# Layer two of two feed-forward parts: where its first rows and operands lie, and which products come last

## The chip, the cores and the metric

The kernel runs on one core of one Trainium2 chip. The metric is the time of one execution on the device in microseconds (us). Only the one core is used, so nothing is exchanged with other cores.

## The reference, cut to what matters

Three transformer-like layers follow each other on a 1024 x 1024 activation in float32. The second ends with a gated feed-forward part, the third with a squared-ReLU one, each followed by a layer norm over the rows (1024 columns):

```python
# second layer
gate_ff, up_ff = jnp.split(x @ w_ffn_in, 2, axis=-1)          # 1024 -> 2 x 2816
ffn = (jax.nn.silu(gate_ff) * up_ff) @ w_ffn_out              # 2816 -> 1024
ple = jax.nn.sigmoid(x @ w_ple_gate) * (p_i @ w_ple_proj)
return _layer_norm(ALPHA * x + ffn + ple, ln2_g, ln2_b)
# third layer begins with x = layer_norm(x, ln_in_g, ln_in_b); its feed-forward part:
ff = jnp.square(jax.nn.relu(jnp.einsum('btd,df->btf', x, w1[l]) + b1[l]))   # 1024 -> 4096
ff = jnp.einsum('btf,fd->btd', ff, w2[l]) + b2[l]                            # 4096 -> 1024
x = layer_norm(DEEPNORM_ALPHA * x + ff, ln2_g[l], ln2_b[l])
```

## The kernel before

Every float32 operand is split into a high and a low part, and each product of two tiles is three matmuls (high by high, high by low, low by high). ScalarE (ACT) makes the high part with a cast, VectorE (DVE) the low one with a subtraction (`part`, L111 and L112, or L485 and L486). The queue of SyncE (SP) issues nearly all DMAs in order.

Both matrix products of a feed-forward part are made by a Winograd scheme: seven half-size products in place of eight, from sums of quarters.

Layer one is `wino_up`. For each unit of 256 columns it makes products 6, 2, 7, 5, 4, 3 and the next unit's 1. Its left operands are the quarters of the activation, which lie in the four tiles of `tpool`, and the sums S1 to S4. S2 and S3 lie in a zone of their own on the right side of SBUF (`Q.zone`, 32 KB a partition) and are read by products 6 and 7; S4, on the left with the staging tiles `h` and `snap`, is read by product 3. The results go through `sink` and `left_parts` to DRAM as `hid`: the seven left operands of layer two, unit by unit.

Layer two is `Down`. The units are taken in groups: 4, 4 and 3 units in the second layer, four groups of 4 in the third. Within a group the products go in the order 1, 6, 7, 4, 5, 3, 2 (`ORDER`). One product is four pieces, one for each 128 rows, of 12 matmuls (9 in the group of 3). A piece accumulates in one PSUM bank. Products 1, 6, 7 and 4 go on in the same four banks, 5 and 3 in four others, 2 in new ones, and after each piece `evict` adds the bank into `acc[m]`: the eight output tiles of 128 rows by 1024 columns. `TO` says which: rows 0 to 3 get products 1, 6, 3 and 2, rows 4 to 7 get 7, 4 and 5. In the last group the pieces of 4 and 5 alternate, as do those of 3 and 2, and the last addition to a row block starts its layer norm: `ln_out` once in the third layer, twice in the second (its own norm, then the norm that the third layer begins with), followed by the transposes into `T5` (L106).

The right operands come from four tiles a, b, c, d for each pair of units (`load`, L616, `ra0` to `rd1`). `combine` forms the sums in place (L440 to L444), and `split` makes the two parts: `a` for product 1, then b := d - b and a := b + a for product 6, b for 7, b := c - a for 4, a := d - a for 5, d for 3 and c for 2. Six weight buffers (`wpool`) hold three products' worth. The left operands are loaded by `left` (L587) from `hid` into raw buffers, two units at a time, and split into a tile of `tpool`. Every second pair goes through a raw buffer of `pl`; in the second layer that is one buffer, which the layer norm's `junk` shares.

At the change-over from layer one to layer two, `early` loads operands of product 1 while the last unit runs, and `later`, called when product 7 of the last unit has freed the zone, loads a to d of group 0 into it. The `acc` tiles lie on the left, where `h`, S4 and `snap` lay, and `fetch` fills them with a DMA from GpSimd's queue (L1618, L2387). In the first addition (L1623, L2399) DVE reads both the bank and `acc`, and the bank's next product waits for it.

The order of the instructions on each engine is fixed when the kernel is built, by a list scheduler that goes by program order and its own estimate of when things are ready. Hence matmuls of product 1 of layer two stand between those of the last unit's products.

Of the kernel before, what the change touches and what calls it, by code (L numbers as in the profile page):

```python
# [10 lines left out]
F32 = mybir.dt.float32  # L11
# [9 lines left out]
D = 1024  # L21
P = 128
NT = S // P
# [8 lines left out]
class Core:  # L32
# [150 lines left out]
def run(gen):  # L183
    for _ in gen:
        pass
# [377 lines left out]
class Down:  # L563
# [42 lines left out]
    def load(self, g):  # L606
        nc, pool = self.c.nc, self.pool
        u0, u1 = self.groups[g]
        parts = [{} for _ in range(u0, u1, 2)]
        for names in ("dba", "c") if g == 0 else ("adbc",):  # L610
            for x, u in enumerate(range(u0, u1, 2)):
                k = min(2, u1 - u)
                for n in names:
                    j, o = {"d": (1, 1), "b": (1, 0), "a": (0, 0), "c": (0, 1)}[n]
                    t = pool.tile([P, 2, 512], F32, name=f"r{n}{x}", tag=f"r{n}{x}", bufs=1)[:, :k]
                    nc.sync.dma_start(t, self.src[j][:, 2 * u + o:2 * (u + k):2])  # L616
                    parts[x][n] = t
        return parts

    def right(self, g):  # L620

        c, nc = self.c, self.c.nc
        parts = self.parts if g == 0 else self.load(g)
        sums = [combine(nc, *(q[n] for n in "abcd")) for q in parts]
# [24 lines left out]

    def run(self, raws, fetch, evict):  # L650

        nc = self.c.nc
        self.raws = raws
        seen = set()
        nG = len(self.groups)
        todo = [(g, n) for g in range(nG) for n in self.ORDER]

        def ahead(i):
            if i < len(todo):
                g, n = todo[i]  # L660
                if (g, n) not in self.A:
                    self.A[g, n] = self.left(n, *self.groups[g])

        def piece(g, n, x, A, W, ps):
            cs = slice(x * P, (x + 1) * P)
            row, j = self.TO[n]
            for k, (wh, wl) in enumerate(W):
                ah, al = A[:, k, cs], A[:, 4 + k, cs]
                nc.tensor.matmul(ps[x], ah, wh, start=n in (1, 5, 2) and k == 0, stop=False, skip_group_check=True)  # L669
# [6 lines left out]
        i = 0  # L676
        fetched = set()
        for g in range(nG):
            rights = self.right(g)
            pair = []  # L680
            for n in self.ORDER:
                W = next(rights)
                ahead(i)
                ahead(i + 1)
                A = self.A.pop((g, n))
                if self.TO[n] not in fetched:
                    fetched.add(self.TO[n])
                    for x in range(4):
                        fetch(4 * self.TO[n][0] + x, self.TO[n][1])
                if n in (1, 5, 2):  # L690
                    new = self.banks()
                if n in (1, 6, 7):
                    ps = new
                if g == nG - 1 and n in (4, 5, 3, 2):

                    pair.append((n, A, W, new if n != 4 else ps))
                    if len(pair) == 2:
                        for x in range(4):
                            for n, A, W, to in pair:
                                piece(g, n, x, A, W, to)  # L700
                        pair = []
                else:
                    for x in range(4):
                        piece(g, n, x, A, W, new if n != 4 else ps)
                i += 1


def block1(c, i, x1_out):
# [751 lines left out]
def block2(c, i, T, x1_scr, x3_scr):  # L1460

    nc, tc = c.nc, c.tc
# [6 lines left out]
    xs_scr = c.dram.tile([NT, P, D], F32, name="xs2", tag="xs2")  # L1469
    ys_scr = c.dram.tile([NT, P, D], F32, name="ys2", tag="ys2")  # L1470
# [21 lines left out]
    def pool(stack, name, side="left", bufs=1):  # L1492
        return stack.enter_context(tc.tile_pool(reuse_waits="tile", name=name, bufs=bufs, side=side))

    with ExitStack() as ctx:
# [52 lines left out]
        down = Down(c, i["w2_ffn_out"], hid, [(0, 4), (4, 8), (8, NFF2)])  # L1548

        def gate(j, halves):  # L1550
# [14 lines left out]
                    nc.sync.dma_start(ys_scr[m][:, cs], x)  # L1565
            return [lambda h=h: steps(h) for h in halves]

        second = []

        def before(whole):  # L1570
# [11 lines left out]
        def sink(v, C):  # L1582
# [18 lines left out]
            else:  # L1601
                have.setdefault("hidden", {})

        wino_up(c, lambda v: i["w2_ffn_in"][v // 2][:, :, 256 * (v % 2):256 * (v % 2) + 256], 0, 2 * NFF2, Q, sink,
                before, meanwhile, down.early, lambda: down.later(pool(ctx, "b2r", "right")))
        uctx.close()

        pl = pool(ctx, "b2l")
        po = pool(ctx, "b2o")
        pa = pool(ctx, "b2a")  # L1610
# [5 lines left out]
        def fetch(m, j):  # L1616
            cs = slice(j * 512, (j + 1) * 512)
# [620 lines left out]
def block3(c, i, T, x3_scr, out):  # L2238
    nc, tc = c.nc, c.tc
# [3 lines left out]
    with ExitStack() as ctx:  # L2243
# [77 lines left out]

    xs_scr = c.dram.tile([NT, P, D], F32, name="xs3", tag="xs3")
    hid = c.dram.tile([7, NFF3, P, 512], F32, name="hid3", tag="hid3")
    with ExitStack() as ctx:
        b1c = pool(ctx, "b3b").tile([P, 32], F32, name="b1c")
        nc.sync.dma_start(b1c, cols["b1_3"])
        with ExitStack() as uctx:
# [37 lines left out]
            def meanwhile(whole):  # L2365
                for u in range(2):
                    whole(u, first[u], 1)
                for u in (2, 3):
# [2 lines left out]
                        whole(u, W, half)  # L2371

            wino_up(c, lambda u: i["w3_1"][u], 4, NFF3, Q, sink, before, meanwhile, down.early,
                    lambda: down.later(pool(ctx, "b3r", "right")))

        pl = pool(ctx, "b3l", "left", bufs=2)
        po = pool(ctx, "b3o")
        pa = pool(ctx, "b3a")
        acc = [pa.tile([P, D], F32, name=f"acc{m}", tag=f"acc{m}") for m in range(NT)]
        rb = {}  # L2380
        sums = {}

        late = [*range(4, NT), *[None] * 4, *range(4)]

        def fetch(m, j):
            cs = slice(j * 512, (j + 1) * 512)
            nc.gpsimd.dma_start(acc[m][:, cs], xs_scr[m][:, cs])  # L2387

        def evict(g, m, j, ps, first, last):
            if g == 1:  # L2390
# [154 lines left out]
```

## Time and profile before

| | |
|---|---|
| median of 3 runs | 3778.19 us (3769.33 to 3781.7) |
| the profiled execution | 3782.46 us, span 3780.8 us |
| PE (matmul) busy | 3528.0 us, 93% |
| PEld (weight load) busy | 2942.5 us, 78% |
| DVE busy | 2237.0 us, 59% |
| ACT busy | 1499.3 us, 40% |
| POOL (GpSimd) busy | 598.0 us, 16% |
| DMA | 445.97 MB, mean 118 GB/s |
| mean granted TensorE clock | 0.961 |

Busy time of PE is modelled and hides pipelining, so what matters is where PE is idle. The slices of the page show it: busy tenths of 9 nearly everywhere, and lower ones in some places.

### The profile page before, as it was taken

What the parts mean: (1) busy time and instruction counts of PE and PEld (TensorE: products, weight loads), DVE (VectorE), ACT (ScalarE), POOL (GpSimd) and SP (SyncE); (2) the same over time, 40 slices, a digit from 0 to 9 for tenths busy, and PEclk for the clock granted to TensorE, in tenths of its full rate; (3) what the DMA queues carried; (4) which work ended last, traced back from release to release, by engine and by line L of the source; (5) the groups of instructions that cost most, each with busy time, mean ns of one, the idle gap of its engine ahead of it and who ended that gap; (6) DMA issues with size and microseconds to landing.
All of it is one profiled execution on the core that took longest, in us unless ns stands there. A gap on an engine that the chain in (4) does not pass through costs nothing.

```text
span 3780.8 us, 49397 instructions
## 1 busy us (share of the span) xinstructions
PE 3528.0 (93%) x18124; PEld 2942.5 (78%) x18124; DVE 2237.0 (59%) x4477; ACT 1499.3 (40%) x3015; POOL 598.0 (16%) x669
## 2 busy tenths in 40 slices
PE   8999999999999899999979769988898989996998
PEld 7788998887989678888858657766777778885887
DVE  5323332256567668565567754475865656666977
ACT  3223232325556444333333443444445344333334
POOL 1000000102223120000000014344434220000200
PEclk9999999999999999999989879998988999998999
DMA  3112112352112365233374224244434343447542
GB/s 129 51 58 77 45 57 73 124 189 70 36 44 73 125 237 195 97 105 99 101 260 143 87 85 134 73 108 115 118 116 144 122 157 128 139 146 274 172 135 78
DMA packets 271666, 445.97 MB, mean 118 GB/s; under 512 B 39456, under 2 KB 141088, under 8 KB 271424
## 3 DMA queue, kind: packets, MB, share of 16 engines
q1 hardware_dynamic: 268864, 434.41, 35.7%
q0 software_dynamic: 2560, 8.39, 0.6%
q8 instruction: 144, 2.36, 0.3%
q14 instruction: 98, 0.80, 0.1%
HBM read 312.37 MB, written 130.35 MB: 117 GB/s over the span
## 4 chain that ended last, share of the span: by engine, by line
PE 77%; DVE 8%; DMA 6%; ACT 3%; issue 2%; POOL 2%; SPq 1%; DVEq 0%; POOLq 0%; ACTq 0%
PE mm L123 8%; PE mm L125 8%; PE mm L124 8%; PE mm L508 3%; PE mm L510 3%; PE mm L509 3%; PE mm L139 3%; PE mm L141 3%; PE mm L140 3%; PE mx L509 2%; PE mx L510 2%; PE mx L508 2%; PE mx L669 2%; PE mx L670 2%; PE mx L671 2%
## 5 line engine op out<-in xcount | busy, mean ns | idle before, releaser
L123 PE MATMUL mm<-w,Thi 128*128 128x512 f32 (+1 forms) x1856 | 659.5, 356 | 10.5 <-ACT Thi L111 3.2
L125 PE MATMUL mm<-w,Tlo 128*128 128x512 f32 (+1 forms) x1856 | 650.1, 351 | 0.0
L124 PE MATMUL mm<-w,Thi 128*128 128x512 f32 (+1 forms) x1856 | 648.8, 350 | 1.0 <-DVE w L68 1.0
L123 PEld LDWEIGHTS mm<-w,Thi 128*128 128x128 f32 x1856 | 353.1, 190 | 58.8 <-ACT Thi L111 5.2
L125 PEld LDWEIGHTS mm<-w,Tlo 128*128 128x128 f32 x1856 | 352.5, 190 | 46.7 <-issue 3.5
L124 PEld LDWEIGHTS mm<-w,Thi 128*128 128x128 f32 x1856 | 353.2, 190 | 44.6 <-issue 2.5
L139 PE MATMUL mm<-Thi,w 128*128 128x512 f32 (+1 forms) x696 | 283.4, 408 | 8.9 <-DVE qo L880 4.0
L140 PE MATMUL mm<-Tlo,w 128*128 128x512 f32 (+1 forms) x696 | 278.7, 400 | 0.0
L141 PE MATMUL mm<-Thi,w 128*128 128x512 f32 (+1 forms) x696 | 277.5, 400 | 0.0
L486 DVE TENSOR_TENSOR w<-wraw,w 128x1024 fp32r<-128x1024 f32 (+1 forms) x136 | 147.9, 1088 | 139.5 <-ACT w L485 139.5
L68 DVE TENSOR_TENSOR w<-wraw,w 128x1024 fp32r<-128x1024 f32 (+2 forms) x96 | 118.5, 1237 | 134.3 <-ACT w L67 133.6
L485 ACT CAST w<-wraw 128x1024 fp32r<-128x1024 f32 (+1 forms) x136 | 128.5, 945 | 173.7 <-PE mm L510 118.7
L67 ACT CAST w<-wraw 128x1024 fp32r<-128x1024 f32 (+1 forms) x139 | 140.7, 1018 | 117.9 <-PE mm L125 20.6
L139 PEld LDWEIGHTS mm<-Thi,w 128*128 128x128 f32 (+1 forms) x696 | 132.8, 191 | 42.1 <-issue 8.5
L141 PEld LDWEIGHTS mm<-Thi,w 128*128 128x128 f32 (+1 forms) x696 | 132.2, 190 | 31.1 <-issue 2.5
L140 PEld LDWEIGHTS mm<-Tlo,w 128*128 128x128 f32 (+1 forms) x696 | 132.4, 190 | 29.7 <-issue 3.0
L112 DVE TENSOR_TENSOR Tlo<-pt,Thi 128x512 fp32r<-128x512 f32 (+2 forms) x144 | 92.3, 656 | 100.8 <-ACT Thi L111 100.1
L669 PE MATMUL mm<-w,Ahl 128*128 128x512 f32 x198 | 79.8, 403 | 75.0 <-DVE acc L2399 28.8
L112 DVE TENSOR_TENSOR Ahl<-wraw,Ahl 128x1024 fp32r<-128x1024 f32 x98 | 119.6, 1224 | 27.0 <-ACT Ahl L111 26.8
L57 POOL TENSOR_TENSOR st<-st,expo 128x1 f32<-128x1 f32 x48 | 37.0, 771 | 581.2 <-DVE st L285 459.8
L68 POOL TENSOR_TENSOR w<-wraw,w 128x1024 fp32r<-128x1024 f32 (+1 forms) x43 | 107.5, 2506 | 123.6 <-ACT w L67 119.4
L111 ACT CAST Thi<-pt 128x512 fp32r<-128x512 f32 (+2 forms) x144 | 77.3, 562 | 123.7 <-PE pt L106 88.5
(660 smaller groups left out, 8572.5 us busy)
## 6 DMA issues: line engine op xcount, KB each, us to landing
hid<-h SPq DMA_DIRECT2D x189, 256.0 KB
wraw<-hid SPq DMA_DIRECT2D x91, 512.0 KB
wraw<-in_w_ffn_in SPq DMA_DIRECT2D x44, 512.0 KB
wraw<-in_w SPq DMA_DIRECT2D x34, 512.0 KB
wraw<-in_w_out SPq DMA_DIRECT2D x28, 512.0 KB
y<-y SPq DMA_DIRECT2D x48, 256.0 KB
rs<-rec_s SPq DMA_DIRECT2D x64, 192.0 KB
xl<-rec_d SPq DMA_DIRECT2D x64, 192.0 KB
```

What stands on the lines that cost most here:

```text
L68: (nc.gpsimd if self.pool_lo else nc.vector).tensor_sub(w[:, 0], raw, w[:, 1].bitcast(F32))
L112: self.nc.vector.tensor_sub(lo, src, hi.bitcast(F32))
L123: nc.tensor.matmul(ps, hi[:, k, cs], wh, start=start and x == 0, stop=False)
L124: nc.tensor.matmul(ps, hi[:, k, cs], wl, start=False, stop=False)
L125: nc.tensor.matmul(ps, lo[:, k, cs], wh, start=False, stop=stop and x == K - 1)
L139: nc.tensor.matmul(ps, wh, hi[:, k0 + k], start=k == 0, stop=False)
L140: nc.tensor.matmul(ps, wh, lo[:, k0 + k], start=False, stop=False)
L141: nc.tensor.matmul(ps, wl, hi[:, k0 + k], start=False, stop=k == K - 1)
L508: nc.tensor.matmul(ps, wh, hi[:, k], start=start and k == 0, stop=False, skip_group_check=True)
L509: nc.tensor.matmul(ps, wh, lo[:, k], start=False, stop=False, skip_group_check=True)
L510: nc.tensor.matmul(ps, wl, hi[:, k], start=False, stop=k == 3, skip_group_check=True)
L669: nc.tensor.matmul(ps[x], ah, wh, start=n in (1, 5, 2) and k == 0, stop=False, skip_group_check=True)
```

## The change

Three things are changed in `Down` and its two callers; layer one is left as it is.

1. `later` puts only d and b of group 0 into the zone of S2 and S3, and beside them `acc` of rows 0 to 3, which are fetched at once, from SP's queue. A new function `room`, called when layer one has ended, puts `acc[4]`, then a and c, then `acc[5]` to `acc[7]` on the left. All fetches now go through SP.
2. In the second layer (`tail=2`) the last two groups run products 1, 6, 7, 4, 5 first, one group after the other, and then 3 and 2 of the first of them, then 3 and 2 of the other. For these late products d and c are loaded a second time. Product 3 no longer finds product 5 in its bank, so product 5 is also added to rows 0 to 3. The third layer keeps its order (`tail=0`).
3. In the second layer all left operands go through the two raw buffers of `rawpool` (`down.run(None, ...)`). `pl` then holds only `junk`.

```diff
-    def later(self, pool):
-        self.pool = pool
-        self.parts = self.load(0)
...
+    def later(self, pool, acc, fetch):
+
+        self.pools = dict.fromkeys("db", pool)
+        self.parts = [{} for _ in self.units(0)]
+        self.load(self.parts, 0, "db")
+        self.fetched = {(0, 0), (0, 1)}
+        for m in range(4):
+            acc[m] = pool.tile([P, D], F32, name=f"acc{m}", tag=f"acc{m}", bufs=1)
+        for j in range(2):
+            for m in range(4):
+                fetch(m, j)
+
+    def room(self, pool, acc):
+
+        self.pools.update(dict.fromkeys("ac", pool))
+        acc[4] = pool.tile([P, D], F32, name="acc4", tag="acc4", bufs=1)
+        self.load(self.parts, 0, "ac")
+        for m in range(5, NT):
+            acc[m] = pool.tile([P, D], F32, name=f"acc{m}", tag=f"acc{m}", bufs=1)
...
-    def right(self, g):
+    def right(self, g, rest):
...
+        if rest:
+            self.load(parts, g, "dc")
+            yield split("d")
+            yield split("c")
+            return
+        if g > 0:
+            self.load(parts, g, "adbc")
+        sums = [combine(nc, *(q[n] for n in "abcd")) for q in parts]
...
-    def run(self, raws, fetch, evict):
+    def run(self, raws, fetch, evict, tail=0):
...
-        todo = [(g, n) for g in range(nG) for n in self.ORDER]
+        whole, late = range(nG - tail), range(nG - tail, nG)
+        todo = [(g, n, False) for g in whole for n in self.ORDER]
+        todo += [(g, n, False) for g in late for n in self.ORDER[:5]]
+        todo += [(g, n, True) for g in late for n in self.ORDER[5:]]
...
-            m = 4 * row + x
-            evict(g, m, j, ps[x], (m, j) not in seen, g == nG - 1 and n in (4, 5, 3, 2))
-            seen.add((m, j))
+            to = [(4 * row + x, j)]
+            if n == 5 and g in late:
+                to.append((x, 1))
+            for m, j in to:
+                evict(g, m, j, ps[x], (m, j) not in seen,
+                      g == nG - 1 and n in (4, 5, 3, 2) and not (n == 5 and m < 4))
+                seen.add((m, j))
...
+            new = n in (1, 5, 2) or rest
...
-        acc = [pa.tile([P, D], F32, name=f"acc{m}", tag=f"acc{m}") for m in range(NT)]
+        down.room(pool(ctx, "b2a"), acc)
...
-            nc.gpsimd.dma_start(acc[m][:, cs], ys_scr[m][:, cs])
+            nc.sync.dma_start(acc[m][:, cs], ys_scr[m][:, cs])
...
-        down.run(pl, fetch, evict)
+        down.run(None, fetch, evict, tail=2)
```

The rest of the diff restates the loop of `run` for the list `todo`, defines `acc` and `fetch` ahead of `wino_up`, and makes the same edits of point 1 in the third layer.

## Rows read from the trace of the kernel before

**Rows 1.** Waits of PE, 1900 to 2230 and 3400 to 3790: total, times, longest us

```profile
PE mm L669 <- DVE acc L1623: 24.8, 1, 24.8
PE mm L669 <- ACT Ahl L111: 21.4, 1, 21.4
...
PE mm L669 <- DVE acc L2399: 28.8, 1, 28.8
```

**Rows 2.** Windows: us, PE, PEld, DVE, ACT, POOL busy, PEclk, DMA share, GB/s

```profile
1928.30:1953.00 24.70, 0.00 (x0) 0.01 (x1) 18.34 (x20) 7.02 (x7) 8.82 (x16) 0.60 1.04 397
2020.00:2096.00 76.00, 76.00 (x337) 62.92 (x336) 55.12 (x64) 25.72 (x29) 0.00 (x0) 1.00 0.41 127
2096.00:2124.60 28.60, 28.60 (x128) 23.69 (x127) 24.85 (x33) 11.16 (x15) 0.00 (x0) 1.00 0.21 74
2124.60:2150.80 26.20, 26.20 (x117) 21.50 (x115) 20.85 (x59) 14.31 (x21) 2.21 (x4) 1.00 0.22 66
2150.80:2176.20 25.40, 3.98 (x12) 3.05 (x12) 16.83 (x40) 13.15 (x21) 2.19 (x4) 0.60 0.38 130
2176.20:2223.70 47.50, 15.18 (x67) 10.29 (x65) 35.60 (x89) 30.42 (x48) 8.52 (x23) 0.60 0.16 55
3442.70:3471.50 28.80, 0.04 (x1) 0.07 (x1) 19.96 (x21) 7.41 (x8) 8.76 (x16) 0.54 0.90 329
```

**Rows 3.** Chain that ended last, at both change-overs: start, us, what

```profile
1936.07 13.89 DMA wraw<-hid
...
1952.20 0.69 DVE acc L1623
...
3455.56 12.83 DMA wraw<-hid
```

**Rows 4.** Timeline of PE at the second layer's change-over

```profile
1916.20 0.40 PE L510 MATMUL mm<-S3h,w 128*128 128x512 f32 x1
...
1924.94 0.40 PE L510 MATMUL mx<-S4h,w 128*128 128x512 f32 x1
...
1953.02 0.76 PE L669 MATMUL mm<-w,Ahl 128*128 128x512 f32 x1 [24.77 <-DVE acc L1623]
```

**Rows 5.** Timelines of SP's and POOL's queues at both change-overs

```profile
1906.60 6.26 SPq L587 DMA_DIRECT2D wraw<-hid  x3
...
1916.63 0.37 SPq L616 DMA_DIRECT2D rd<-in_w_ffn_out  x1
...
1928.20 4.56 POOL L1618 DMA_DIRECT2D acc<-ys  x8 [503.27 <-DMA rc<-in_w_ffn_out]
...
3430.82 0.38 SPq L616 DMA_DIRECT2D rd<-in_w  x1
```

**Rows 6.** Timelines of DVE and ACT: making operands of product 6

```profile
1932.66 1.22 DVE L441 TENSOR_TENSOR ra<-rb,ra 128x1024 f32<-128x1024 f32 x1
...
1933.91 1.05 ACT L111 CAST w<-ra 128x1024 fp32r<-128x1024 f32 x1 [0.71 <-DVE ra L441]
...
1935.54 1.22 DVE L112 TENSOR_TENSOR w<-ra,w 128x1024 fp32r<-128x1024 f32 x1
...
3452.21 1.21 DVE L112 TENSOR_TENSOR Ahl<-wraw,Ahl 128x1024 fp32r<-128x1024 f32 x1
```

**Rows 7.** Timelines of DVE, PE and ACT at the second layer's end

```profile
2124.57 0.68 DVE L1631 SCALAR_TENSOR_TENSOR acc<-acc,mm 128x512 f32<-128x512 f32 x1
...
2172.39 0.80 PE L669 MATMUL mm<-w,Ahl 128*128 128x512 f32 x1 [21.42 <-ACT Ahl L111]
...
2198.14 1.15 ACT L284 ACTIVATE junk<-acc,st 128x1024 f32<-128x1024 f32 x1
...
2207.91 1.15 ACT L284 ACTIVATE junk<-acc,st 128x1024 f32<-128x1024 f32 x1
...
2223.74 0.80 PE L139 MATMUL mx<-Thi,w 128*128 128x512 f32 x1
```

**Rows 8.** Waits of ACT in layer two of the second layer, 1955 to 2125

```profile
ACT Ahl L111 <- DMA wraw<-hid: 24.6, 8, 8.0
```

More of the change, by code (lines that the diff above doesn't have):

```diff
@@ L599, in early @@
             self.W1 += [(w[:, 1, y], w[:, 0, y]) for y in range(k)]
-    def later(self, pool):
-        self.pool = pool
-        self.parts = self.load(0)
-    def load(self, g):
-        nc, pool = self.c.nc, self.pool
-        u0, u1 = self.groups[g]
[L609 to L618, printed above, removed]
@@ new lines, in units, with load @@
+    def units(self, g):
+        u0, u1 = self.groups[g]
+        return [(u, min(2, u1 - u)) for u in range(u0, u1, 2)]
+    def load(self, parts, g, names):
+        for x, (u, k) in enumerate(self.units(g)):
+            for n in names:
+                j, o = {"d": (1, 1), "b": (1, 0), "a": (0, 0), "c": (0, 1)}[n]
+                t = self.pools[n].tile([P, 2, 512], F32, name=f"r{n}{x}", tag=f"r{n}{x}", bufs=1)[:, :k]
+                self.c.nc.sync.dma_start(t, self.src[j][:, 2 * u + o:2 * (u + k):2])
+                parts[x][n] = t
@@ L622, in right @@
+    def right(self, g, rest):
         c, nc = self.c, self.c.nc
-        parts = self.parts if g == 0 else self.load(g)
-        sums = [combine(nc, *(q[n] for n in "abcd")) for q in parts]
+        parts = self.parts if g == 0 else [{} for _ in self.units(g)]
         def split(n):
@@ L655, in run, with piece @@
         nG = len(self.groups)
-        todo = [(g, n) for g in range(nG) for n in self.ORDER]
+        whole, late = range(nG - tail), range(nG - tail, nG)
+        todo = [(g, n, False) for g in whole for n in self.ORDER]
+        todo += [(g, n, False) for g in late for n in self.ORDER[:5]]
+        todo += [(g, n, True) for g in late for n in self.ORDER[5:]]
         def ahead(i):
             if i < len(todo):
-                g, n = todo[i]
+                g, n, _ = todo[i]
                 if (g, n) not in self.A:
                     self.A[g, n] = self.left(n, *self.groups[g])
-        def piece(g, n, x, A, W, ps):
+        def piece(g, n, x, A, W, ps, new):
             cs = slice(x * P, (x + 1) * P)
@@ L668, in piece @@
                 ah, al = A[:, k, cs], A[:, 4 + k, cs]
-                nc.tensor.matmul(ps[x], ah, wh, start=n in (1, 5, 2) and k == 0, stop=False, skip_group_check=True)
+                nc.tensor.matmul(ps[x], ah, wh, start=new and k == 0, stop=False, skip_group_check=True)
                 nc.tensor.matmul(ps[x], ah, wl, start=False, stop=False, skip_group_check=True)
                 nc.tensor.matmul(ps[x], al, wh, start=False, stop=k == len(W) - 1, skip_group_check=True)
-            m = 4 * row + x
@@ L673, in piece @@
-            evict(g, m, j, ps[x], (m, j) not in seen, g == nG - 1 and n in (4, 5, 3, 2))
-            seen.add((m, j))
[L676 to L687, printed above, removed]
-                    for x in range(4):
[L689 to L705, printed above, removed]
@@ new lines, in piece @@
+            to = [(4 * row + x, j)]
[5 more added lines that the diff above has]
+                seen.add((m, j))
+        pair = []
+        for i, (g, n, rest) in enumerate(todo):
+            if n == (3 if rest else 1):
+                rights = self.right(g, rest)
+            W = next(rights)
+            ahead(i)
+            ahead(i + 1)
+            A = self.A.pop((g, n))
+            if self.TO[n] not in self.fetched:
+                self.fetched.add(self.TO[n])
+                for x in range(4):
+                    fetch(4 * self.TO[n][0] + x, self.TO[n][1])
+            new = n in (1, 5, 2) or rest
+            if new:
+                banks = self.banks()
+            if n == 1:
+                chain = banks
+            one = (g, n, A, W, chain if n == 4 else banks, new)
+            if g == nG - 1 and n in (4, 5, 3, 2):
+                pair.append(one)
+                if len(pair) == 2:
+                    for x in range(4):
+                        for g, n, A, W, to, new in pair:
+                            piece(g, n, x, A, W, to, new)
+                    pair = []
+            else:
+                for x in range(4):
+                    piece(g, n, x, *one[2:])
@@ L1566, in gate, with fetch @@
             return [lambda h=h: steps(h) for h in halves]
+        acc = {}
+        def fetch(m, j):
+            cs = slice(j * 512, (j + 1) * 512)
+            nc.sync.dma_start(acc[m][:, cs], ys_scr[m][:, cs])
         second = []
@@ L1604, in block2 @@
         wino_up(c, lambda v: i["w2_ffn_in"][v // 2][:, :, 256 * (v % 2):256 * (v % 2) + 256], 0, 2 * NFF2, Q, sink,
-                before, meanwhile, down.early, lambda: down.later(pool(ctx, "b2r", "right")))
+                before, meanwhile, down.early, lambda: down.later(pool(ctx, "b2r", "right"), acc, fetch))
         uctx.close()
@@ L2323, in block3, with fetch @@
     hid = c.dram.tile([7, NFF3, P, 512], F32, name="hid3", tag="hid3")
+    acc = {}
+    def fetch(m, j):
+        cs = slice(j * 512, (j + 1) * 512)
+        nc.sync.dma_start(acc[m][:, cs], xs_scr[m][:, cs])
     with ExitStack() as ctx:
@@ L2373, in block3 @@
             wino_up(c, lambda u: i["w3_1"][u], 4, NFF3, Q, sink, before, meanwhile, down.early,
-                    lambda: down.later(pool(ctx, "b3r", "right")))
+                    lambda: down.later(pool(ctx, "b3r", "right"), acc, fetch))
         pl = pool(ctx, "b3l", "left", bufs=2)
         po = pool(ctx, "b3o")
-        pa = pool(ctx, "b3a")
-        acc = [pa.tile([P, D], F32, name=f"acc{m}", tag=f"acc{m}") for m in range(NT)]
+        down.room(pool(ctx, "b3a"), acc)
         rb = {}
@@ L2383, in block3 @@
         late = [*range(4, NT), *[None] * 4, *range(4)]
-        def fetch(m, j):
-            cs = slice(j * 512, (j + 1) * 512)
-            nc.gpsimd.dma_start(acc[m][:, cs], xs_scr[m][:, cs])
         def evict(g, m, j, ps, first, last):
```

3 lines of the change are left out of this document (removed).

## The prediction

> **What bounds the kernel now.** I read the page first. PE is busy 93% of the span and the chain that ended last runs through it, so the edits can only pay where PE stands still. The waits of PE around the two feed-forward parts [rows 1] name three such places: 24.8 us before layer two of the second layer, 28.8 us before that of the third, both ended by an addition into `acc` on DVE, and 21.4 us near the second layer's end, ended by the cast of a left operand. Inside the groups PE waits for nothing. The windows [rows 2] then say what else was going on. In the first gap (1928.3 to 1953.0) the DMA engines are full, at 397 GB/s, and DVE is busy 18.3 of 24.7 us; in the second it is 329 GB/s and 20.0 of 28.8 us. At the second layer's end, from 2124.6 to 2223.7, PE does 45.4 us of work in 99.1 while DVE does 73.3: there the layer norms set the pace. After each gap the clock is at its lower level for a few microseconds.
>
> **Change-over of the second layer.** The chain [rows 3] ends in a hid transfer of 13.89 us from 1936.07, its cast and split, and behind that on DVE the first `acc` addition at 1952.20, upon which product 6 starts at 1953.02 [rows 4]. The fetches stand on POOL's queue from 1928.20, after the operands of the zone, which were issued from 1916.63 [rows 5], when product 7's last read of S3, at 1916.20, had freed it [rows 4]. After the change `acc` of rows 0 to 3 is issued there in place of a and c, so it is no longer late. What is late next is a, since product 6 needs a + (d - b). It lies over S4, whose last reader ends at 1924.94 plus 0.4 us [rows 4], so SP can issue it from 1925.4.
>
> When it lands I work out from bytes. From 1916.6 on come d and b (2 MiB), four `acc` tiles (2 MiB), about three hid stores of 0.25 MiB, about one hid load of 0.5 MiB, and a, c, a (1.5 MiB): 6.75 MiB or 7.1 MB. At the 0.39 to 0.40 MB per us of the gap [rows 2] that is 18 us, and I add some 2 us for the start: the second a lands near 1937, the first 2.7 us before. Addition, cast and low part take 1.22, 1.05 and 1.22 us [rows 6], 3.5 in all: weights at 1938 and 1940.5. The first half keeps PE busy for the 2.5 us between. So PE resumes near 1938 and the gap is 10 us instead of 24.7: **-14 us**. The left operands are no obstacle: both raws of product 6 now go through `rawpool`, where three hid loads were issued as early as 1906.6 to 1912.9 [rows 5]. Bounds: -2 us if a comes as late as the last hid load did, -26 if nothing is missing (the gap and a microsecond or two of slow clock).
>
> **Change-over of the third layer.** The same edit, with the operands issued from 3430.82 [rows 5]. The same bytes with one more hid load and store (7.9 MB) need 20 us at that rate; with the start the second a lands near 3453, the first near 3450, so product 6 could begin near 3453.5. Its left operand, which here still goes through `pl`, had its low part begun at 3452.21 [rows 6]; behind other traffic I put it 2 us later. PE resumes near 3454.5, 12 us after 3442.7 instead of 28.8: **-17 us**, bounds -3 and -30.
>
> **Does the queue itself matter?** The rows show the first gap's DMA engines full while transfers from POOL's queue and from SP's are under way together [rows 2, 5]. The Trainium skill, page "DMA: Bandwidth & Descriptors", section "Issuing engines are not separate DMA queues", says that DMAs started by any engine run on the same 16 engines, so that another issuer saves only issue time. By that rule point 1 moves no fewer bytes and would give back almost nothing; the sum would be the tail's -21 us alone, 3757 us. I hold against it that the order changes: 2 MiB of `acc` for rows 4 to 7, and whatever else comes behind a, are no longer ahead of what product 6 needs. It is a rival below.
>
> **Order of the last groups.** A group of four is 336 matmuls, 76.0 us [rows 2], so 0.226 us each. Products 3 and 2 of the middle group are 96 matmuls, 21.7 us, that move from ahead of the last rows-4-to-7 products to behind them. The layer norms of rows 4 to 7 therefore begin 21.7 us earlier against the same PE work, the first now at 2124.57 [rows 7].
>
> How long the norms last then is the question. One row goes every 9.8 us: 2198.14 to 2207.91 between equal steps [rows 7], since the squares share one `junk`. Eight rows are 78 us, plus a start and an end of about 6: 84 us is the floor. DVE gives a second bound. It has 73.3 us of work in the 99.1 [rows 2]. To that come two products' splits and additions: each has four low parts of 1.22 and four additions of 0.69 (durations as in [rows 3, 6]), 7.6 us, so 15.3; and four more additions of product 5, 2.8 us. That is 91 us. In the first half, until row 7 is through, DVE would have 37.7 + 18 = 56 us to do in the 51.6 it took before, so that half does not get shorter. The second half loses its 21.4 us stall of PE, which came from the raw buffer shared with `junk` [rows 1], but it stood in the shadow of the norms of rows 4 to 7 and cost only the three microseconds or so between their end and the first of rows 0 to 3. I take the stretch as 99 to 100 us as before: **-21 us**. Bounds: 84 us of norms gives -36; a stretch 15 us longer gives -6.
>
> **What I cost at nothing.** The second load of d and c is 3.5 MiB, 9.4 us of DMA, under groups that move 127 and 74 GB/s [rows 2]. The eight additions (5.5 us) hide under PE, as DVE has 55.1 us of work in 76.0 and 24.9 in 28.6. In the middle group's first pass it falls to 55.1 - 15.3 + 2.8 = 42.6 us for 54 of PE; in the last group's the cover is thin, and all 2.8 us would show if it went. SP gets 32 fetches and eight loads more at 0.4 to 0.5 us each; what stands behind them on its queue are hid loads and stores, which wait longer for their buffers than that. POOL loses its fetches and nobody waits for it.
>
> **Sum.** -14 - 17 - 21 = -52 us: 3782.5 becomes 3730.5 for the profiled execution. It stood 4.3 us above the median of the runs, so I predict **3726 us**.
>
> **Rivals.** *The same bytes, the same gap.* The change-overs are bound by what must land, a and c simply take the place of `acc`, and DVE's 18 to 20 us of work in each gap keeps PE waiting; both give 3 us, the tail 21: 3751 us. For it: full DMA engines. Against it: in the third layer the left operand of product 6 was ready around 3453.5, 18 us before PE went on. *DVE bounds the last groups.* The last group's first pass, DVE at 87% already, slips, and the norms stretch with it; the tail gives 2 us: 3745 us. For it: 91 us of DVE in a stretch of 99. Against it: half of that stretch had DVE at 75%. *The edits cancel or do nothing,* as the order of instructions is the scheduler's: 3778 us. *Slower: two raw buffers instead of three.* Every product of the second layer's groups now sends both its raws through two buffers, whose turn (issue 0.4, landing, two casts, two low parts) must fit in 10.9 us, in 8.2 in the last group. ACT already waited 24.6 us for hid loads there, 8.0 at most [rows 8]. With a landing of 13.9 us as in the change-over [rows 3] the turn is near 19, and nineteen products would lose up to 8 us each. It decides from 3.3 us a product on, 63 us in all, past the 52 gained: about 3790 us at that point and more beyond. Against it: the groups use 0.41 and 0.21 of the DMA engines, and left tiles are made up to two products ahead.
>
> **How the numbers follow.** Forecast 0.62; same bytes 0.16; DVE-bound groups 0.10; no effect 0.05; slower 0.07. The likeliest case by itself spans its sum with half of the way to each bound: 3706 to 3747. The range of 3703 to 3764 takes in both middle rivals and a tail of -6 with poor change-overs (-14 in all, upper end), and at the lower end change-overs of -17 and -22 with the 84 us floor. About 11 us (0.3%) is what a measurement of this kernel tells from no change. All cases but the last two are faster by more than that, less a little of the weak ends: faster 0.86, same 0.07, slower 0.07.
>
> **What would show it.** Right: PE's waits before product 6 at 8 to 14 us in both layers, ended by a weight split behind a, no longer by an `acc` addition; fetches on SP in the zone's place right after d and b; no wait of 21 us for a cast near the end; the first norm's square some 36 us earlier (21.7 and 14) and the third layer's first matmul about 35. Wrong: waits at the change-overs that hardly shrank; PE idle inside the last two groups; ACT waiting for hid loads in every product; or a stretch from the first norm to the third layer's first matmul that is far from 99 us.

## The result, and the profile after

The changed kernel takes 3744.66 us (median of 4 runs, 3736.78 to 3752.25) against 3776.6 of before in the same job: ratio 0.9917, 95% interval 0.989 to 0.9943. It is faster, by 32 us where 52 were forecast, and inside the range. The profiled execution took 3745.23 us, with a span of 3743.5 (before: 3780.8).

PE's waits of the changed kernel around the two parts (total, times, longest us), which answer to [rows 1]:

```profile
PE mm L694 <- ACT w L111: 17.5, 1, 17.5
...
PE mm L694 <- ACT w L111: 15.9, 1, 15.9
```

Both waits before product 6 shrank, from 24.8 to 17.5 and from 28.8 to 15.9, and their ender is now the cast of a weight that is made from a, as forecast; the `acc` additions are no longer last. The 21.4 us wait for a left operand near the second layer's end is gone.

The windows of the changed kernel, with the columns of [rows 2]: the two gaps, the two halves of the second layer's last stretch, and ten microseconds inside the first half:

```profile
1932.60:1950.10 17.50, 0.00 (x0) 0.00 (x0) 11.39 (x15) 4.18 (x4) 0.00 (x0) 0.62 0.93 341
3417.50:3433.40 15.90, 0.04 (x2) 0.01 (x1) 8.48 (x13) 2.09 (x2) 0.00 (x0) 0.63 0.94 334
...
2100.80:2160.00 59.20, 53.65 (x239) 43.68 (x237) 53.17 (x121) 33.81 (x48) 5.14 (x7) 0.96 0.37 122
2160.00:2208.70 48.70, 12.46 (x49) 8.78 (x49) 34.37 (x87) 30.14 (x48) 8.26 (x20) 0.50 0.22 75
...
2110.00:2120.00 10.00, 10.00 (x46) 8.29 (x45) 10.00 (x19) 7.42 (x10) 0.00 (x0) 1.00 0.31 96
```

In the second layer's gap the DMA engines are no longer full (0.93 and 341 GB/s, 1.04 and 397 before), and in the two gaps DVE stands idle for some 6 and 7 us. In the last stretch it is the other way round: PE has 53.7 and DVE 53.2 us of work in the 59.2 of the first half, and in 2110 to 2120 both are busy without a break.

Timelines of the changed kernel's PE, SP, DVE and ACT around the second layer's change-over:

```profile
1928.75 0.40 PE L510 MATMUL mx<-S4h,w 128*128 128x512 f32 x1
1950.11 1.22 PE L694 MATMUL mm<-w,Ahl 128*128 128x512 f32 x2 [17.53 <-ACT w L111]
...
1938.46 1.05 SPq L453 DMA_DIRECT2D hid<-h  x2
1941.48 0.37 SPq L587 DMA_DIRECT2D wraw<-hid  x1
1942.25 0.38 SPq L630 DMA_DIRECT2D ra<-in_w_ffn_out  x1
...
1940.23 1.22 DVE L112 TENSOR_TENSOR Ahl<-wraw,Ahl 128x1024 fp32r<-128x1024 f32 x1 [1.07 <-ACT Ahl L111]
1942.11 1.23 DVE L112 TENSOR_TENSOR Ahl<-wraw,Ahl 128x1024 fp32r<-128x1024 f32 x1 [0.65 <-ACT Ahl L111]
1946.61 1.23 DVE L112 TENSOR_TENSOR Ahl<-wraw,Ahl 128x1024 fp32r<-128x1024 f32 x1 [3.28 <-ACT Ahl L111]
1947.75 1.22 DVE L441 TENSOR_TENSOR ra<-rb,ra 128x1024 f32<-128x1024 f32 x1
1950.04 1.23 DVE L441 TENSOR_TENSOR ra<-rb,ra 128x1024 f32<-128x1024 f32 x1 [1.07 <-DMA ra<-in_w_ffn_out]
...
1949.01 1.04 ACT L111 CAST w<-ra 128x1024 fp32r<-128x1024 f32 x1 [2.43 <-DVE ra L441]
```

S4 is free at 1929.15, but SP issues a only at 1942.25: on its queue stand hid stores, and loads that wait for a raw buffer. On DVE the sum a + (d - b) (line 441) comes behind three low parts `Ahl`, each of which waits for the cast of a hid load. Counted along the loads, product 6's two were through by 1920.4 and product 7's by 1934.8; these three are for products 4 and 5, which PE reaches 20 us later and more. The sum starts in the instant in which the last of them ends. When the first a had landed the trace doesn't show; the second one kept DVE waiting for 1.07 us.

In the third layer what came last was a itself, by its turn on SP's queue. Timelines of PE, SP and DVE there:

```profile
3414.41 0.39 PE L510 MATMUL mx<-S4h,w 128*128 128x512 f32 x1
...
3425.62 0.42 SPq L630 DMA_DIRECT2D ra<-in_w  x1
...
3431.03 1.23 DVE L441 TENSOR_TENSOR ra<-rb,ra 128x1024 f32<-128x1024 f32 x1 [5.81 <-DMA ra<-in_w]
```

a is issued 10.8 us behind S4's last read, and DVE stands idle for 5.81 us until it lands; no low part of a later product is in the way.

At the second layer's end the first last-addition starts on DVE, row 5's two squares (each row has two norms) stand on ACT, and the third layer's first matmul follows on PE:

```profile
2100.78 0.68 DVE L1660 SCALAR_TENSOR_TENSOR acc<-acc,mx 128x512 f32<-128x512 f32 x1
...
2117.92 1.15 ACT L284 ACTIVATE junk<-acc,st 128x1024 f32<-128x1024 f32 x1
2134.44 1.15 ACT L284 ACTIVATE junk<-acc,st 128x1024 f32<-128x1024 f32 x1
...
2208.66 0.79 PE L139 MATMUL mx<-Thi,w 128*128 128x512 f32 x1
```

From first to last of these it is 107.9 us, against 99.1 between 2124.57 and 2223.74 [rows 7]. Windows, with the columns of [rows 2]: from row 4's first square to row 0's in the changed kernel, the same in the kernel before, and the changed kernel's ten microseconds behind layer two's last matmul (it ends at 2151.13):

```profile
2104.60:2163.20 58.60, 51.52 (x230) 41.98 (x228) 51.90 (x116) 35.41 (x51) 5.14 (x7) 0.93 0.34 113
...
2126.20:2177.80 51.60, 29.20 (x122) 23.41 (x120) 37.80 (x97) 28.41 (x41) 4.40 (x8) 0.80 0.28 96
...
2151.20:2161.60 10.40, 3.32 (x17) 2.05 (x16) 10.40 (x21) 6.03 (x10) 0.00 (x0) 0.69 0.54 173
```

**Where the 37.3 us between the two spans lie,** cut at PE's rows: start to the second layer's layer one +3.8 and that layer +0.5 (code unchanged); wait at the second change-over -7.2; from there to the third layer's first matmul -12.2; the third layer up to its change-over -10.1 (code unchanged); wait there -12.9; the rest +0.8. The three changed places give 32.3, close to what the medians show (31.9).

### The profile page after: what moved, and what is told of

It reads as the page before. It is cut to its first block, busy times and chain, and to the rows that moved or that the text cites. A ratio compares the mean times of both kernels' runs of the same rounds, so it can differ in the third digit from the quotient of the medians.

```text
span 3743.5 us, 49400 instructions
## 1 busy us (share of the span) xinstructions
PE 3526.8 (94%) x18124; PEld 2941.3 (79%) x18124; DVE 2237.6 (60%) x4485; ACT 1500.5 (40%) x3015; POOL 586.5 (16%) x637
## 3 DMA queue, kind: packets, MB, share of 16 engines
q8 instruction: 144, 2.36, 0.3%
## 5 line engine op out<-in xcount | busy, mean ns | idle before, releaser
L112 DVE TENSOR_TENSOR Ahl<-wraw,Ahl 128x1024 fp32r<-128x1024 f32 x98 | 119.4, 1224 | 15.9 <-ACT Ahl L111 15.9
L111 ACT CAST Ahl<-wraw 128x1024 fp32r<-128x1024 f32 x98 | 95.9, 1015 | 49.4 <-DMA wraw<-hid 37.2
```

The source lines that it names most:

```text
L111: self.nc.scalar.copy(hi, src)
L112: self.nc.vector.tensor_sub(lo, src, hi.bitcast(F32))
```

## The experiments

Every experiment ran in five rounds beside the kernel before, and its ratio is to those runs (medians 3777.6 to 3782.7 us). The two waits are PE's before product 6 (second and third layer); "groups" is the time from PE's start in the second layer's groups after the wait to the third layer's first matmul; "third" the time from there to the start of the third layer's wait. These four come from one profile each.

| kernel | median us | ratio to before [95%] | wait 2 | groups | third | wait 3 |
|---|---|---|---|---|---|---|
| before | 3776.6 | 1 | 24.8 | 270.7 | 1218.9 | 28.8 |
| after | 3744.7 | 0.9917 [0.989, 0.9943] | 17.5 | 258.6 | 1208.9 | 15.9 |
| E1 a, c on GpSimd's queue | 3741.2 | 0.9909 [0.9893, 0.9925] | 22.5 | 258.5 | 1192.2 | 26.5 |
| E2 change-overs only | 3759.5 | 0.9954 [0.9937, 0.9971] | 15.6 | 272.5 | 1210.2 | 16.7 |
| E3 order and raws only | 3762.1 | 0.9967 [0.9954, 0.9981] | 24.8 | 259.0 | 1214.5 | 28.7 |
| E4 two raws only | 3763.7 | 0.9966 [0.9952, 0.9981] | 24.4 | 268.0 | 1203.1 | 30.0 |
| E5 two junk buffers | 3744.0 | 0.9894 [0.9877, 0.991] | 17.3 | 259.0 | 1205.0 | 16.0 |
| E6 three groups' ends | 3742.7 | 0.9895 [0.9875, 0.9914] | 17.8 | 251.7 | 1214.9 | 17.3 |
| E7 third layer only | 3765.5 | 0.9963 [0.9949, 0.9978] | 25.3 | 270.5 | 1216.9 | 16.5 |
| E8 gate | 3736.3 | 0.9882 [0.9867, 0.9896] | 13.4 | 258.4 | 1213.3 | 11.8 |
| E9 gate and GpSimd's queue | 3728.7 | 0.9862 [0.9844, 0.9879] | 8.8 | 258.6 | 1211.5 | 11.2 |
| E10 low parts on GpSimd | 3748.5 | 0.9918 [0.9898, 0.9938] | 17.2 | 264.2 | 1210.2 | 16.6 |
| E11 E9 and E10 | 3722.0 | 0.9848 [0.9828, 0.9868] | 8.9 | 263.5 | 1196.7 | 10.7 |
| E12 E9 and E6 | 3710.5 | 0.982 [0.9806, 0.9833] | 8.9 | 249.2 | 1201.8 | 10.8 |

**E1: a and c of group 0 on GpSimd's queue.** The changed kernel with

```diff
-        self.load(self.parts, 0, "ac")
+        self.load(self.parts, 0, "ac", self.c.nc.gpsimd)
...
-                self.c.nc.sync.dma_start(t, self.src[j][:, 2 * u + o:2 * (u + k):2])
+                (queue or self.c.nc.sync).dma_start(t, self.src[j][:, 2 * u + o:2 * (u + k):2])
```

> The changed kernel with one edit: a and c of group 0 are issued from GpSimd's queue instead of SP's. Theory (order on SP's queue): in the changed kernel a was issued 12 us after its room was free, behind hid loads and stores that waited on SP; on an empty queue it is issued when S4 has been read, so PE's wait before product 6 falls from 17.5 to about 8 us in the second layer and from 15.9 to about 8 us in the third, some 17 us in all. Rival (bytes): the DMA engines are what is short, a lands no earlier, both waits stay within 2 us of what they were.

The waits grew, to 22.5 and 26.5 us: the theory that SP's queue alone holds product 6 back fell. Timelines of E1's POOL, SP, ACT and DVE at the second layer's change-over:

```profile
1928.81 0.94 POOL L630 DMA_DIRECT2D ra<-in_w_ffn_out  x1 [500.60 <-DVE h L1631]
...
1932.20 0.37 SPq L587 DMA_DIRECT2D wraw<-hid  x1
...
1943.35 1.04 ACT L111 CAST Ahl<-wraw 128x1024 fp32r<-128x1024 f32 x1 [15.85 <-DMA wraw<-hid]
...
1944.43 1.23 DVE L112 TENSOR_TENSOR Ahl<-wraw,Ahl 128x1024 fp32r<-128x1024 f32 x1 [6.09 <-ACT Ahl L111]
1946.32 1.22 DVE L112 TENSOR_TENSOR Ahl<-wraw,Ahl 128x1024 fp32r<-128x1024 f32 x1 [0.67 <-ACT Ahl L111]
1950.74 1.23 DVE L112 TENSOR_TENSOR Ahl<-wraw,Ahl 128x1024 fp32r<-128x1024 f32 x1 [3.20 <-ACT Ahl L111]
1951.88 1.22 DVE L441 TENSOR_TENSOR ra<-rb,ra 128x1024 f32<-128x1024 f32 x1
...
DMA to landing us min/median/max: 7.3/8.4/9.5
```

a is issued at 1928.81, 0.3 us behind S4's last read (13.1 in the changed kernel), and the two loads of a land within 9.5 us of their issue (last line), by about 1940. But the sum starts at 1951.88, later still. It stands behind the same three low parts, and the hid load for the first of them, issued at 1932.20 behind a and c, now takes till 1943.35. What was hurried arrived, and what stood ahead of it in DVE's order was pushed back. In the third layer it is the same: the sum starts at 3429.09 behind three low parts, with a issued at 3402.54. This gave the theory that E8 and E9 test. E1's total is no worse than the changed kernel's, as its untouched stretch ("third") is 16.7 us shorter.

**E2, E3, E4: one part of the change alone.** E2 is the changed kernel with the old order and raws (`down.run(pl, fetch, evict)`); E3 is the changed kernel with `acc`, its fetches and a, c where the kernel before has them; E4 is the kernel before with `down.run(None, fetch, evict)` in the second layer.

> The changed kernel with the old order of the groups (tail 0) and the raw buffer of pl again in the second layer; only the change-overs are new. Theory (the three parts add up): about 20 us faster than the kernel before (7 and 13 at the two waits), and the end of the second layer as before, with the wait of 21 us for a cast back and some 99 us from the first norm to the third layer's first matmul. Rival (the parts hang together): less than 10 us or more than 28 us.

> The changed kernel with the change-overs of the kernel before (a to d in the zone, acc on the left, fetched by GpSimd); only the order of the last two groups and the two raw buffers are new. Theory: waits before product 6 back at about 25 and 29 us; the norms start 21 us earlier in the stage but their stretch lasts about 108 us instead of 99, so about 12 us faster than the kernel before. Rival (the longer stretch came from the change-overs, as fetches or loads in the way): the stretch is 99 us and the gain 21 us.

> The kernel before with one edit: in the second layer all left operands go through the two raw buffers of rawpool, so junk no longer shares one with them. Theory: PE's wait of 21 us near the end goes, but it lay in the shadow of the norms, so the time falls by 3 us or less beyond what the change-over moves. Rival 1 (the wait was on the path): 15 to 21 us faster. Rival 2 (two buffers are too few): ACT waits for hid loads in most products, PE stands still in the groups, slower by 10 us or more.

The parts act where they should, and by themselves: E2 has the short waits (15.6 and 16.7) and the old groups, E3 the old waits (24.8 and 28.7) and the new groups (259.0). The stretch from the first last-addition to the third layer's first matmul is 99.5 us in E2 and 108.0 in E3, as expected. E4, two raw buffers alone, loses the 21.4 us wait for the cast, and its groups get 2.7 us shorter, about the three microseconds that the prediction gave for that wait; nothing in them shows the 3.3 us a product at which the slower rival would have decided. Most of E4's gain (12.8 us by its ratio, between the outcomes named) lies in the third layer, where its code is that of before.

**E5: two junk buffers** (`junk = pl.tile([P, D], mybir.dt.bfloat16, name="junk", tag="wraw", bufs=2)`).

> The changed kernel with two junk buffers (bf16, so that both fit in the place of one) for the squares of the second layer's layer norms, whose output nobody reads. The stretch from the first last-addition to the third layer's first matmul was 99.2 us before and is 107.9 after the change. Theory A, that DVE's work sets the first half (rows 4 to 7, with DVE full from 2110 to 2120) and the squares' single junk buffer the second (9.8 us a row): the second half gets shorter, the first hardly: the stretch falls to 95 to 102 us, and the kernel gains 6 to 12 us over the changed one, ratio to before near 0.989. Theory B, that DVE sets both halves: no change within 3 us, 0.9917.

Groups of 259.0 us: no change. With two buffers the rows 0 to 3 still follow each other every 9.6 to 9.9 us on ACT (2168.73, 2178.65, 2188.29 and 2197.92; 9.8 with one). So it isn't the shared buffer that paces them, as the prediction had it. Timeline of E5's ACT:

```profile
2168.73 1.15 ACT L284 ACTIVATE junk<-acc,st 128x1024 bf16<-128x1024 f32 x1 [1.32 <-DVE st L283]
...
2169.88 1.13 ACT L284 ACTIVATE junk<-acc,st 128x1024 bf16<-128x1024 f32 x1
```

By the program's order the first of these is row 0's second square and the other row 1's first. That one waits for nothing, as the last addition to rows 0 to 3 began at 2147.46; it stands behind the other in ACT's order. So each step holds one pass of a row's chain from DVE to ACT, GpSimd and back, and the next row starts only with the next pass. Whether another order of the rows would be shorter was not tested. The ratio of 0.9894, near what theory A named, is luck: groups and waits are those of the changed kernel, and so is its median (3744.0).

**E6: products 3 and 2 of all three groups at the end** (`tail=3`).

> The changed kernel with products 3 and 2 of all three groups of the second layer at the end, not of the last two: another 96 matmuls, 21.7 us, move behind the first last-addition, and the norms of rows 4 to 7 begin some 21 us earlier. Theory A, that after the change the first half of the last stretch (rows 4 to 7, 59.2 us) is full, as it holds 53.7 us of PE and 53.2 of DVE: moved products now lengthen the stretch by almost what the norms start earlier; the stretch goes from 108 to 124 to 130 us, the gain over the changed kernel is 0 to 5 us, ratio to before about 0.991. Theory B, that the norms still set the pace and every group moved is worth its 20 us: a stretch of 108 to 110 us and 3725 us, ratio 0.986.

The first last-addition starts at 2075.0, and the stretch behind it takes 121.2 us, with 87.8 of PE and 101.4 of DVE in it. The groups get 6.9 us shorter, a little more than the first theory allowed and a third of what the second asked. So 21.7 us of products under the norms gave 12 us the first time (with the two raw buffers, which alone gave 2.7 in E4) and 7 the second.

**E7: the third layer's change-over alone,** the second layer as before.

> The kernel before with the new change-over in the third layer alone; the second layer is untouched, and on every engine the instructions stand in the order of before up to the third layer's change-over. In the kernels run so far the stretch from the third layer's first table load to the start of PE's wait at the third change-over lasted between 1191 and 1218 us, although its code is the same in all. Theory 1, that this spread comes with the order of instructions, which the scheduler of the build makes anew whenever something ahead of it is changed: here the stretch is that of before, 1218 us within 3, the wait falls from 28.8 to about 16, and the kernel gains 13 us, ratio 0.9966. Theory 2, that the spread is from run to run or follows from the change itself: the stretch lies nearer 1205, and the gain is 20 us or more, ratio 0.994 or less.

PE's waits of E7 at the third change-over, where the kernel before has 28.8:

```profile
PE mm L839 <- ACT w L111: 16.5, 1, 16.5
```

The wait, the stretch ahead of it (1216.9) and the gain (ratio 0.9963) are those of the first theory.

**E8: the left operand of product 4 behind the sum.** The changed kernel with

```diff
+            if gate is not None:
+                c.nc.vector.tensor_copy(raw[:, 0, 0:1], gate[:, 0, 0:1])
             c.nc.sync.dma_start(raw, self.hid[LEFT.index(OF[n]), u:u + k].rearrange("u p n -> p u n"))
...
+                    gate = self.parts[-1]["a"] if (g, n) == (0, 4) else None
```

> The changed kernel, but the hid loads for the left operand of product 4 in group 0 wait for the sum a + (d - b) of the second operand tile (a copy of one column on DVE, 0.1 us each, makes them wait). In the changed kernel and in the one with a and c on GpSimd's queue, DVE has the low parts of left operands for products 4 and 5 ahead of that sum in its order, although these are used more than 20 us later. Theory A, that this order and SP's queue keep PE waiting: with those loads gone a is issued right behind the six hid stores, near 1939.5 in place of 1942.25, lands some 5.5 us later, and the sum no longer waits for anything else: PE's waits fall from 17.5 and 15.9 by about 3 us each, to 14 and 13, ratio to before about 0.990. Theory B, that the bytes that have to land set the wait whatever their order: 17.5 and 15.9 as they were, 0.9917.

Waits of 13.4 and 11.8: theory A, by a little more than it asked. The gate takes the loads off SP's queue and their low parts out of DVE's order at once, so in the second layer E8 doesn't part the two. Timelines of E8's SP and DVE:

```profile
1925.13 8.46 SPq L453 DMA_DIRECT2D hid<-h  x6
1933.68 0.40 SPq L632 DMA_DIRECT2D ra<-in_w_ffn_out  x1
...
1932.55 0.69 DVE L472 TENSOR_TENSOR h<-h 128x512 f32<-128x512 f32 x1
1937.73 1.23 DVE L441 TENSOR_TENSOR ra<-rb,ra 128x1024 f32<-128x1024 f32 x1 [4.49 <-DMA ra<-in_w_ffn_out]
```

a now follows the six hid stores directly, DVE has nothing ahead of the sum, and the sum waits for a's landing alone, 4.05 us behind its issue.

**E9: the gate, GpSimd's queue for a and c, and rawpool alone in the third layer** (E8 with E1's edit, and `down.run(None, fetch, evict)` there too).

> The same gate, with a and c of group 0 issued on GpSimd's queue as in the first of the experiments, and the third layer's groups through the two raw buffers of rawpool alone, so that no hid load of product 6 waits for the zone. Theory A: a is issued within a microsecond of the zone's last read, lands some 9 us later, and since neither SP's queue nor a low part of a later product stands ahead of the sum, PE waits 8 to 10 us at both change-overs (22.5 and 26.5 with GpSimd's queue alone); against the changed kernel some 15 us less, if the third layer's stretch ahead of its change-over keeps its length. Theory B, the bytes: the DMA engines are full from the first operands on, and the waits stay at 15 or more. A third possibility: the gated loads come too late for product 4, and PE stands still there in place of here.

Waits of 8.8 and 11.2, the second a little above theory A, and PE waits nowhere for product 4. POOL's and DVE's timelines and the windows of both gaps of E9:

```profile
1924.31 0.94 POOL L632 DMA_DIRECT2D ra<-in_w_ffn_out  x1 [500.71 <-DVE h L1634]
...
1933.06 0.69 DVE L472 TENSOR_TENSOR h<-h 128x512 f32<-128x512 f32 x1
1933.67 1.22 DVE L441 TENSOR_TENSOR ra<-rb,ra 128x1024 f32<-128x1024 f32 x1
...
1927.18:1936.02 8.84, 0.00 (x1) 0.00 (x1) 7.69 (x12) 1.04 (x1) 0.24 (x1) 0.69 1.04 405
3406.08:3417.23 11.15, 0.00 (x1) 0.01 (x1) 9.76 (x14) 1.04 (x1) 0.54 (x1) 0.61 1.04 395
```

The sum waits for nothing: DVE comes to it straight from its work on `h`, and is busy for 7.7 of the 8.8 us. The DMA engines are full again, yet the gap is half as long, since what product 6 doesn't need comes later. The same early issue that lengthened the wait in E1 shortens it here by 4.6 us in the second layer (E8 to E9). In the third, where the raw buffers changed as well, it gives 0.6 (11.8 to 11.2): DVE is busy for 9.8 of the 11.2 us.

**E10: the late products' low parts on GpSimd.** The changed kernel with `c.part(..., nc.gpsimd if rest else None)` for both operands of the late products 3 and 2.

> The changed kernel with the low parts of the operands of the late products 3 and 2 (both groups of the second layer, some 15 of 1.22 us on DVE) on GpSimd, where one takes some 2.5 us and which is idle there. Theory A, that DVE is what stretched the first half from 51.6 to 58.7 us, row 4's square to row 0's: the half gets shorter by some 4 us, down to PE's 53.7 us of work, and the stretch from the first last-addition to the third layer's first matmul falls from 107.9 to 103 or 104. Theory B, that PE's moved products or the chain of a row set it: no change within 2 us. Slower, if GpSimd's low parts come too late for the last products: PE then waits for them inside the last groups.

The groups got 5.6 us longer, and PE doesn't wait inside them; none of the three outcomes named. POOL's and DVE's timelines and a window of E10 show why:

```profile
2117.18 3.64 POOL L112 TENSOR_TENSOR w<-rd,w 128x1024 fp32r<-128x1024 f32 x2
2120.79 1.07 POOL L57 TENSOR_TENSOR st<-st,expo 128x1 f32<-128x1 f32 x2
2121.84 2.40 POOL L112 TENSOR_TENSOR Ahl<-wraw,Ahl 128x1024 fp32r<-128x1024 f32 x1
...
2115.28 0.15 DVE L285 TENSOR_SCALAR st<-st 128x1 f32<-128x1 f32 x1 [1.12 <-ACT junk L284]
2117.99 0.69 DVE L1668 TENSOR_TENSOR acc<-acc,mx 128x512 f32<-128x512 f32 x1 [1.97 <-PE mx L696]
2121.90 2.36 DVE L287 TENSOR_TENSOR st<-st 128x1 f32<-128x1 f32 x1 [0.36 <-POOL st L57]
2124.18 4.67 DVE L290 TENSOR_TENSOR acc<-acc,bc 128x512 f32<-128x512 f32 x2
...
2110.00:2120.00 10.00, 10.00 (x46) 8.28 (x45) 5.00 (x12) 4.67 (x9) 10.00 (x6) 1.00 0.49 155
```

The norms' own step on GpSimd (line 57, 0.55 us) is ready after 2115.43 and starts at 2120.79, behind low parts; and two of DVE's products with a row vector (line 290) take 4.67 us together beside GpSimd's work, 1.28 in the changed kernel. DVE was relieved (5.0 us in 2110 to 2120, 10.0 in the changed kernel), and the rows went slower all the same. So the run doesn't tell whether DVE's load by itself stretched the first half; it shows that a delay in a row's chain does.

**E11 and E12: combinations.**

> The gate, GpSimd's queue for a and c and rawpool alone (8.8 and 11.2 us of waits at the change-overs, 3728.7 us before) together with the low parts of the late products on GpSimd. If theory A of the run before holds, 3 to 4 us less than with the gate and the queue alone, near 3725, ratio to before 0.985; if not, 0.986 to 0.987.

> The gate, GpSimd's queue for a and c and rawpool alone, with products 3 and 2 of all three groups at the end. If the two findings stand beside each other: waits of 9 and 11 us at the change-overs, 251 to 253 us from PE's start in the second layer's groups to the third layer's first matmul (258.6 with two groups at the end), and some 7 us less than the 3728.7 us with two: near 3722, ratio to before 0.9845, give or take 10 us for the third layer's stretch ahead of its change-over, whose order the build makes anew. If the earlier start of the groups and the later norms want the same DVE time, the 258 us stay and the kernel is at 3728.

E11's time is near what its first theory said, but not for its reason: its groups are as long as E10's (263.5), and what it gains over E9 lies in the third layer (1196.7). E12 has both findings at once, waits of 8.9 and 10.8 and groups of 249.2, and is the fastest, at 0.982 of before against 0.9917 for the change. It is 11.5 us below what was expected; 9.7 us of its gain over E9 lie in the untouched stretch (1201.8 against 1211.5).

## Why the prediction was right, and where its sizes were off

- **Direction and places: right.** Less waiting at both change-overs, no wait of 21 us for a cast, the norms earlier, and each part for itself (E2, E3). The sizes were not: the three terms gave 32.3 of the 52 us, the waits lay above the 8 to 14 us named as a sign, and the third layer's first matmul came 15.1 us earlier, not 35. The time fell inside the range because the range was wide; it is also the 3745 us of the rival with DVE-bound groups, which had other parts (31 from the change-overs, 2 from the groups).
- **Change-overs, -14 and -17: measured -7.2 and -12.9.** The step that failed is "SP can issue it from 1925.4". I had reckoned the landing of a from the moment at which its place is free, and not from its turn on SP, 13.1 us later; and "the left operands are no obstacle" looked at product 6's alone, while in the second layer those of products 4 and 5 stood ahead of the sum on DVE. In the third DVE was free and waited for a, which SP issued 10.8 us behind S4's last read. With both obstacles away (E9) the waits are 8.8 and 11.2, where the forecast had 10 and 12. There a lands 7 to 10 us after its issue, where the forecast had put the two loads some 9 and 12 us behind S4's last read, so its bytes and rate were about right. That the waits agree so well is in part luck: in E9 DVE's other work ends them, which the sum had left out.
- **Order of the last groups, -21: measured -12.2.** The term failed at "the stretch as 99 to 100 us as before"; it became 107.9. I had seen that DVE's first half wouldn't get shorter, but not that it would get longer (row 4's square to row 0's: 58.7 us, 51.6 before), though my own 56 us of DVE work in 51.6 said so. And I had not counted PE in it: with the moved products PE has 51.5 us of work in that half, where it had 29.2. PE is busy for 0.88 of it and DVE for 0.89. The trace speaks for DVE as the cause and against PE: DVE waited for PE 2.7 us in that half (4.6 before), and was busy without a break for the ten microseconds behind layer two's last matmul. Row 4's second norm, for one, has its sums at 2113.0, but its next step on DVE starts at 2116.4, behind two low parts and two additions. No run shows it by an edit: E10 relieved DVE, but delayed the rows on GpSimd.
- **The rivals.** "The same bytes, the same gap" is refuted by E9, though DVE's work, its second reason, is what is left of the gap there. The Trainium skill, page "DMA: Bandwidth & Descriptors", section "Issuing engines are not separate DMA queues", would have another issuer save only issue time; E1 agrees in that it gained nothing at the gaps, and E8 to E9 shows what an issue 9.8 us earlier (10.1 us behind S4's last read in E8, 0.3 in E9) is worth once nothing else stands ahead: 4.6 us. That is time in which the load stood in SP's queue, not the time that its issue takes (0.4 us), so here the measurement goes beyond the rule. "DVE bounds the last groups" was half right: 9 of the 21 us went there, not 19. "Two raw buffers" cost nothing that shows (E4).
- **Costed at nothing:** inside the groups PE waits for nothing in the changed kernel either; DVE's work in 2020 to 2096 rose from 55.1 to 62.7 us of 76 and stayed hidden.

## What to carry to other kernels

When a load's buffer comes free earlier, work out its issue from its queue: what stands ahead of it there, and what those wait for; then do the same on the engine that takes the data. An operand that is made far ahead of its use costs nothing until its load is late, and then everything behind it in that engine's order is late too. And work that is moved under a stretch that another engine paces is not free: add up every engine's work in that stretch, half by half, before you call it hidden.

## What the runs showed beyond this

**A stretch whose code nobody touched takes 1192 to 1219 us.** In the traces PE's 4520 matmuls from the third layer's first one to layer one of its feed-forward part stand in the same order in before, E7 and E9, and the stretch takes 1218.9, 1216.9 and 1211.5 us. E4 and E11 share another order, with 1203.1 and 1196.7. In the changed kernel the order is that of before up to the 1115th of them, and in all other kernels it differs too: 1192.2 to 1214.9. The scheduler makes the order anew for each build. So kernels of one order lie within some 7 us of each other, and the two orders at least 8 us apart; with one profile for each kernel, how much of that is spread from run to run stays open. It means that a total here carries some 10 us that are not the edit's, so the edits were judged by their own places.

**GpSimd's elementwise work holds up DVE's.** In E10 two DVE products of SBUF tiles of 128x512 took 4.67 us together while GpSimd was on its low parts, 1.28 without; the addition from PSUM beside the same work kept its 0.69. It isn't a matter of size: a product of one column (line 287) took 2.36 us there, 0.16 in the changed kernel, and it ended with GpSimd's instruction of 2.40 us that had begun 0.06 us before it (E10's rows at 2121.84 and 2121.90). The Trainium skill, page "GPSIMD Engine Reference", section "1. Specifications", says that GpSimd shares its SBUF interfaces with VectorE, with contention for DVE instructions with two SBUF inputs; the rows agree with that.
